# Moving scale and shift of the first norm behind the turn, for four of eight blocks

## The chip, the cores and the metric

The kernel runs on one core of a Trainium2 chip. The metric is the device time of one execution in microseconds (us). An execution under the profiler leaves a trace: every instruction of the engines TensorE (PE, its weight loads PEld), VectorE (DVE), ScalarE (ACT), GpSimd (POOL) and of SyncE's (SP) queue, which issues most transfers, with its start and end.

## The reference, cut to what matters

One layer of a decoder trunk on x of 1024 tokens by 1024 channels, in float32:

```python
x = _layer_norm(ALPHA * x + mixed, ln1_g, ln1_b)      # first norm
hid = silu(x @ w_ffn_gate) * (x @ w_ffn_up)           # 2816 hidden channels
x = _layer_norm(ALPHA * x + hid @ w_ffn_down, ln2_g, ln2_b)
```

`mixed` is the output of three branches (a state-space model, a gated recurrence, an attention), gated, summed and multiplied by `w_out`. A norm takes mean and variance over the 1024 channels of a token, divides, and then multiplies by a scale and adds a shift for each channel. The first norm's output is used twice: as the input of the two gate matrices, and as the residual of the second norm.

## The kernel before, in words

Every float32 operand of a product is split into a high and a low part, and a product is three matmuls (`mm3`, line 117 through `mm`). ScalarE casts the high part, VectorE subtracts to get the low part (`split`, lines 143 and 129). The three stages that matter here:

**Mix stage** (`mix_out`, from line 944). Tokens lie in eight blocks of 128, on the partitions; channels lie along a row. For each block `tb` and each half `dh` of the channels, 24 matmuls fill a PSUM bank, VectorE adds `ALPHA * x` and measures mean and variance (`measure`). After the second half `norm` (line 927) runs on VectorE: two passes subtract the mean and multiply by the scale row `g1`, a reciprocal, two passes multiply by 1/sigma and add the shift row `b1`. The scale and shift rows are broadcast to all partitions, since here a channel is a column. The result goes to DRAM (`x1_d`, through ScalarE's queue).

**Turn** (`turn`, from line 978). The gate stage needs channels on the partitions. TensorE transposes a normalised block in eight 128x128 pieces into two banks, `pa[0]` (channels 0 to 511) and `pa[1]` (512 to 1023). Blocks 0 to 3 are kept. Blocks 4 to 7 are combined with them into the operands `x22`, `s1` to `s4` of a seven-product scheme (Strassen's): ScalarE copies `pa[1]` to `x22`, VectorE subtracts and adds with `pa[0]` read straight from PSUM, VectorE or GpSimd does the other sums, and each operand is split (`operand`, line 970). Program order is: the second halves of blocks 4 to 7, each from block 5 on followed by the turn of the block before it; block 7 is turned inside the gate stage (line 1141), after three rounds of two products. The first product that needs an operand made from all of blocks 4 to 7 comes with `middle(0)`, line 1148.

**Down stage** (from line 1178). It multiplies the hidden values by `w_ffn_down`, in 7 products of 11 steps each, 12 matmuls a step. For each step SyncE loads two halves, ScalarE casts them and VectorE subtracts (`factors`); four such pairs of buffers exist, and three steps are prepared ahead. `residual(tb)` loads a block of the first norm's output back from `x1_d`; `scaled` multiplies it by ALPHA and adds a product; `finish` does the second norm, where ScalarE already subtracts the mean and divides in one pass (`Identity` with a scale and a bias for each partition).

What sets the order: a planner simulates the program and orders each engine's instructions by readiness and program order. From the gate stage on, compute instructions are pinned (`pin`): they keep their program order on their engine. Transfers are not pinned and are issued as early as their buffers and their queue allow. The down stage's buffers (`row`, `r`, `p3`) lie where those of the gate stage were, and wait for them.

Of the kernel before, what the change touches and what calls it, by code (L numbers as in the profile page):

```python
# [16 lines left out]
AF = mybir.ActivationFunctionType  # L17
ALU = mybir.AluOpType
# [3 lines left out]
P = 128  # L22
# [35 lines left out]
def trunk(ctx: ExitStack, tc: tile.TileContext, A: dict, out: bass.AP):  # L58
# [20 lines left out]

    LATE = {  # L80
        "ws": ("keep", 4), "w": ("keep", 8), "x": ("keep", 9), "m8": ("mid", 4), "ln": ("mid", 2),
        "mx": ("right", 8), "wo": ("right", 4), "r": ("down", 8), "row": ("down", 2), "p3": ("down", 22),
    }
    pinned = [False]
    count = [0]
# [12 lines left out]
    def small(shape, dt=F32, name_="c"):  # L98
        return const.tile(list(shape), dt, name=name(name_))
# [363 lines left out]
    PE.transpose(pr[:, 0:124], rows, ident[0:124, 0:124])  # L463
    cols = small([P, 124], name_="cols")
    DVE.tensor_copy(cols, pr[:, 0:124])
    half = small([P, 60], name_="half")
    ts(DVE, half, cols[:, 0:60], 0.5, ALU.mult)

# [458 lines left out]
    def norm(r, tb, g, b, ready=lambda dh: None):  # L927

        mv, rs = few("mv", [P, 4], 2, "const"), few("rs", [P, 1], 2, "const")
        pin(DVE.bn_aggr(mv[:, 0:2], stats.pop(tb)[:, :, 0:6]))  # L930
        pin(ACT.activation(rs, mv[:, 1:2], AF.Sqrt, bias=eps_t))
        for dh in range(2):
            pin(stt(r[dh], r[dh], mv[:, 0:1], g[dh], ALU.subtract, ALU.mult))
        pin(DVE.reciprocal(rs, rs))
        for dh in range(2):
            pin(stt(r[dh], r[dh], rs, b[dh], ALU.mult, ALU.add))
            ready(dh)

    def halves_of(t):
        return [t[:, 512 * dh : 512 * dh + 512] for dh in range(2)]  # L940

# [2 lines left out]
    def mix_out(tb, dh):  # L944
        h, c = tb // 4, slice((tb % 4) * P, (tb % 4 + 1) * P)
        if dh == 0:
            acc[tb] = new("x")
            SP.dma_start(acc[tb], x_in[tb * P : (tb + 1) * P, :])
        r = halves_of(acc[tb])
        ps = bank(tag="ba"[tb % 2])  # L950
        for k in range(NK):
            q, kk = k // 4, k % 4
            mm3(ps, MH[h][q][:, kk, c], ML[h][q][:, kk, c], WO[dh][q][0][:, kk, :], WO[dh][q][1][:, kk, :], k == 0, k == NK - 1)
        stt(r[dh], r[dh], ALPHA, ps, ALU.mult, ALU.add)
        measure(r[dh], tb, dh)
        if dh == 1:
            norm(r, tb, g1, b1)
            ACT.dma_start(x1_d[tb], acc[tb])


# [17 lines left out]
    def turn(tb, place, e=POOL):  # L978
        j = tb % 4
        pa = []  # L980
        for q in range(2):
            pa.append(place(q))
            for k in range(4):
                PE.transpose(pa[q][:, k, :], acc[tb][:, (4 * q + k) * P : (4 * q + k + 1) * P], ident)
        if tb < 4:
            raw[j] = new("x", shape=(P, 8, P))
            ACT.copy(raw[j][:, 0:4], pa[0])
            DVE.tensor_copy(raw[j][:, 4:8], pa[1])
            operand("x11", j, raw[j][:, 0:4], DVE)
            operand("x12", j, raw[j][:, 4:8], POOL)  # L990
            return
        xs, s1 = new("x", shape=(P, 8, P)), new("x", shape=(P, 8, P))[:, 0:4]
        x22, s2, s3, s4 = xs[:, 0:4], xs[:, 4:8], raw[j][:, 0:4], raw[j][:, 4:8]
        ACT.copy(x22, pa[1])
        tt(DVE, s3, s3, pa[0], ALU.subtract)
        tt(DVE, s1, pa[0], x22, ALU.add)
        tt(e, s2, x22, s3, ALU.subtract)
        tt(e, s4, s4, s2, ALU.subtract)
        operand("x22", j, x22, DVE)
        operand("s3", j, s3, DVE)  # L1000
        operand("s2", j, s2, e)
        operand("s1", j, s1, DVE)
        operand("s4", j, s4, e)
# [209 lines left out]
    def residual(tb):  # L1213
        t = new("r", shape=(P, D))
        SP.dma_start(t, x1_d[tb])
        whole[tb], res[tb] = t, halves_of(t)

    def scaled(tb, dh, e):
        pin(stt(res[tb][dh], res[tb][dh], ALPHA, e, ALU.mult, ALU.add))
# [3 lines left out]
        pin(measure(res[tb][dh], tb, dh))  # L1223

    def finish(tb, last=False):
        g2, b2 = rows_
        if last:
            norm(res[tb], tb, halves_of(g2), halves_of(b2), lambda dh: SP.dma_start(out[tb * P : (tb + 1) * P, 512 * dh : 512 * dh + 512], res[tb][dh]))
            return
        r = whole[tb]  # L1230
        mv, rs = few("mv", [P, 4], 2, "const"), few("rs", [P, 1], 2, "const")
        nm = mv[:, 2:3]
        pin(DVE.bn_aggr(mv[:, 0:2], stats.pop(tb)[:, :, 0:6]))
        pin(ACT.activation(rs, mv[:, 1:2], AF.Sqrt, bias=eps_t))
        pin(DVE.reciprocal(rs, rs))
        pin(ts(DVE, nm, mv[:, 0:1], rs, ALU.mult, -1.0, ALU.mult))
        pin(ACT.activation(r, r, AF.Identity, bias=nm, scale=rs))  # L1237
        tt(DVE, r, r, g2, ALU.mult)
        tt(POOL, r, r, b2, ALU.add)
        SP.dma_start(out[tb * P : (tb + 1) * P, :], r)  # L1240
# [59 lines left out]
    def measured(tb, dh):  # L1300
        pin(measure(res[tb][dh], tb, dh))

    for n in ("ln2_g", "ln2_b"):
        t = new("row", shape=(P, D))
        SP.dma_start(t, A[n].rearrange("(a d) -> a d", a=1).broadcast_to([P, D]))
        rows_.append(t)
# [43 lines left out]
```

## Time and profile before

| | us |
|---|---|
| median of 3 runs | 1650.58 (1650.56 to 1651.05) |
| the profiled execution | 1650.19 |
| its span, first to last instruction | 1648.4 |
| PE busy | 1592.8 |
| DVE busy | 1011.6 |
| ACT busy | 634.5 |
| POOL busy | 599.5 |

The mean granted clock of TensorE is 0.989 of full speed. Times in the rows are counted from the start of the span. The mix stage ends at 991, the gate stage runs from there to about 1424, the down stage to the end. In a row, the names are tiles without their numbers: `x` is a work tile, `ln` a broadcast row of the first norm, `mx`, `wo`, `m` hold split operands, `w` a split weight or hidden factor, `r` a residual block, `row` a broadcast row in the down stage, `p`, `a`, `b` are PSUM banks. `x3` at the end means three instructions merged into a row, the first figure their start and the second their length together.

### The profile page before, as it was taken

The page shows a single profiled execution, that of the slowest core. Times are in us where ns is not written, and L with a number is a line of the kernel's source. Part 1 is how long each engine was busy: PE and PEld are TensorE (multiplying, and loading weights), DVE is VectorE, ACT ScalarE, POOL GpSimd, SP SyncE. Part 2 cuts the span into 40 slices and gives each one's busy share as a digit, 9 for nine tenths or more (in the row PEclk, how much of TensorE's full clock was granted, in tenths as well). Part 3 has the DMA queues.
Part 4 walks back from the last instruction along what each step waited for, and adds up shares of the span by engine and source line. Part 5 has one row for each costly group of instructions (what it writes and reads, how often), then busy time and mean ns, then how long its engine had stood idle before and what let it go on. Part 6 is the DMA issues. An engine that isn't in the chain of part 4 may idle for free.

```text
span 1648.4 us, 20516 instructions
## 1 busy us (share of the span) xinstructions
PE 1592.8 (97%) x7482; PEld 1321.1 (80%) x7482; DVE 1011.6 (61%) x1602; ACT 634.5 (38%) x960; POOL 599.5 (36%) x529
## 2 busy tenths in 40 slices
PE   8989999999899999999999998999999999999997
PEld 6877888877787888888888886788888888778886
DVE  4756575723643467887657769666555555547766
ACT  4425454524633445564213224223222222244442
POOL 0111316333143011112040028599987888400004
PEclk9999999999999999999999998999999999999999
DMA  5343324333332333344754712356544455597752
GB/s 169 76 102 80 80 78 105 77 79 100 88 83 67 116 116 113 114 144 169 246 185 162 244 49 77 126 193 200 171 166 166 154 177 170 202 331 233 245 174 102
DMA packets 219968, 236.09 MB, mean 143 GB/s; under 512 B 33376, under 2 KB 162524, under 8 KB 219868
## 3 DMA queue, kind: packets, MB, share of 16 engines
q1 hardware_dynamic: 192604, 202.83, 39.5%
q10 hardware_dynamic: 27264, 31.96, 5.9%
q8 instruction: 59, 0.97, 0.2%
q14 instruction: 41, 0.34, 0.1%
HBM read 163.96 MB, written 70.78 MB: 142 GB/s over the span
## 4 chain that ended last, share of the span: by engine, by line
PE 78%; DVE 9%; issue 4%; DMA 3%; ACT 3%; POOL 2%; SPq 1%; ACTq 0%; DVEq 0%; POOLq 0%
PE b L117 35%; PE p L117 32%; PE a L117 8%; PE s L117 2%; PE a L341 1%; DMA ws<-w_ffn_down 1%; POOL s L129 1%; DVE r L129 1%; DVE s L129 1%; DVE x L137 1%; DVE wo L129 1%; DMA nck<-ck_d 1%; DVE m L129 1%; DVE x L129 1%; ACT r L1237 1%
## 5 line engine op out<-in xcount | busy, mean ns | idle before, releaser
L117 PE MATMUL b<-x,wh 128*128 128x512 f32 x912 | 351.9, 397 | 2.3 <-ACT s L708 1.7
L117 PE MATMUL b<-x,wl 128*128 128x512 f32 x832 | 328.5, 395 | 0.0
L117 PE MATMUL b<-m,wh 128*128 128x512 f32 x784 | 309.1, 394 | 0.0
L117 PE MATMUL p<-mx,w 128*128 128x512 f32 x1056 | 250.0, 392 | 2.1 <-DVE mx L129 1.3
L117 PEld LDWEIGHTS p<-mx,w 128*128 128x128 f32 x1056 | 199.7, 189 | 44.4 <-issue 1.7
L117 PEld LDWEIGHTS b<-x,wh 128*128 128x128 f32 x912 | 172.9, 190 | 37.4 <-ACT s L708 2.0
L117 PEld LDWEIGHTS b<-x,wl 128*128 128x128 f32 x832 | 157.4, 189 | 31.7
L129 DVE TENSOR_TENSOR x<-x,p 128x512 f32<-128x512 f32 x163 | 108.4, 683 | 109.4 <-PE p L117 92.5
L117 PEld LDWEIGHTS b<-m,wh 128*128 128x128 f32 x784 | 148.8, 190 | 28.7 <-issue 0.2
L117 PE MATMUL p<-w,w 128*128 128x512 f32 x528 | 157.4, 390 | 1.1 <-DVE w L129 1.0
L129 POOL TENSOR_TENSOR s<-s,s 128x1024 f32<-128x1024 f32 (+9 forms) x76 | 77.2, 1015 | 207.4 <-ACT s L852 75.2
L129 DVE TENSOR_TENSOR w<-ws,w 128x1024 fp32r<-128x1024 f32 x88 | 116.0, 1324 | 51.8 <-ACT w L143 51.6
L143 ACT CAST w<-ws 128x1024 fp32r<-128x1024 f32 x88 | 92.1, 1050 | 103.4 <-PE p L117 64.0
L117 PE MATMUL p<-wo,w 128*128 128x512 f32 x528 | 127.3, 389 | 0.0
L129 DVE TENSOR_TENSOR wl<-ws,wh 128x1024 fp32r<-128x1024 f32 x62 | 85.8, 1383 | 65.5 <-ACT wh L143 62.2
L117 PEld LDWEIGHTS p<-w,w 128*128 128x128 f32 x528 | 98.8, 188 | 22.9 <-DVE w L129 2.6
L117 PEld LDWEIGHTS p<-wo,w 128*128 128x128 f32 x528 | 99.1, 188 | 20.5
L143 ACT CAST wh<-ws 128x1024 fp32r<-128x1024 f32 x62 | 65.1, 1050 | 125.0 <-PE b L117 99.2
L129 DVE TENSOR_TENSOR w<-m,w 128x1024 fp32r<-128x1024 f32 x44 | 69.0, 1567 | 63.2 <-ACT w L143 63.2
L129 POOL TENSOR_TENSOR ln<-x,x 128x512 f32<-128x512 f32 x44 | 75.7, 1727 | 63.6 <-ACT x L1172 52.2
L117 PE MATMUL p<-w 128*128 128x512 f32 x264 | 97.5, 390 | 1.1 <-ACT w L143 1.1
L129 POOL TENSOR_TENSOR r<-r,row 128x1024 f32<-128x1024 f32 x7 | 16.7, 2391 | 189.5 <-DVE r L129 184.3
(276 smaller groups left out, 2721.6 us busy)
## 6 DMA issues: line engine op xcount, KB each, us to landing
ws<-w_in SPq DMA_DIRECT2D x48, 512.0 KB, 4.1
ws<-w_ffn_gate SPq DMA_DIRECT2D x27, 512.0 KB, 4.2
gate_d<-zs ACTq DMA_DIRECT2D x48, 256.0 KB, 2.0
zs<-gate_d SPq DMA_DIRECT2D x48, 256.0 KB, 2.8
ws<-w_ffn_up SPq DMA_DIRECT2D x22, 512.0 KB, 4.6
x<-w_ffn_down SPq DMA_DIRECT2D x22, 512.0 KB, 5.6
hid_d<-ln SPq DMA_DIRECT2D x22, 512.0 KB, 3.9
wts_d<-x SPq DMA_DIRECT2D x22, 512.0 KB, 2.6
```

Of the source, the lines that this page charges most:

```text
L117: PE.matmul(o, a, b, start=first, stop=last)
L129: return pin(e.tensor_tensor(o, a, b, op))
L137: return DVE.scalar_tensor_tensor(out=o, in0=a, scalar=s, in1=b, op0=op0, op1=op1)
L143: pin(ACT.copy(hi, src))
L341: PE.transpose(ta[:, j, e, :], pts[e][:, (k0 + j) * P : (k0 + j + 1) * P], ident)
L1237: pin(ACT.activation(r, r, AF.Identity, bias=nm, scale=rs))
```

## The change

Blocks 4 to 7 are normalised without scale and shift: a new function `center`, cut out of `finish`, does mean and 1/sigma with one pass of ScalarE, and `mix_out` calls it for these blocks in place of `norm`. What is stored in `x1_d` for them has no scale and shift. They are applied in two places. In `turn`, a channel is a partition, so ScalarE applies them as it reads the eight transposed pieces from PSUM, one instruction of 128x128 each, with the scale and shift of that piece as one value for each partition (`gain1`, `bias1`, loaded at the start with channels on the partitions); the first half goes to a new tile `x21`. In `residual`, GpSimd multiplies and adds the broadcast rows, which the down stage now loads as well (four `row` tiles instead of two). Blocks 0 to 3 are as before.

```diff
--- before.py
+++ after.py
@@ -79,7 +79,7 @@
 
     LATE = {
         "ws": ("keep", 4), "w": ("keep", 8), "x": ("keep", 9), "m8": ("mid", 4), "ln": ("mid", 2),
-        "mx": ("right", 8), "wo": ("right", 4), "r": ("down", 8), "row": ("down", 2), "p3": ("down", 22),
+        "mx": ("right", 8), "wo": ("right", 4), "r": ("down", 8), "row": ("down", 4), "p3": ("down", 22),
     }
     pinned = [False]
     count = [0]
@@ -463,6 +463,9 @@
     PE.transpose(pr[:, 0:124], rows, ident[0:124, 0:124])
     cols = small([P, 124], name_="cols")
     DVE.tensor_copy(cols, pr[:, 0:124])
+    gain1, bias1 = [small([P, 32], name_="gain")[:, 0:NK] for _ in range(2)]
+    for t, n in ((gain1, "ln1_g"), (bias1, "ln1_b")):
+        SP.dma_start(t, A[n].rearrange("(k p) -> p k", p=P))
     half = small([P, 60], name_="half")
     ts(DVE, half, cols[:, 0:60], 0.5, ALU.mult)
 
@@ -936,6 +939,16 @@
             pin(stt(r[dh], r[dh], rs, b[dh], ALU.mult, ALU.add))
             ready(dh)
 
+    def center(r, tb):
+
+        mv, rs = few("mv", [P, 4], 2, "const"), few("rs", [P, 1], 2, "const")
+        nm = mv[:, 2:3]
+        pin(DVE.bn_aggr(mv[:, 0:2], stats.pop(tb)[:, :, 0:6]))
+        pin(ACT.activation(rs, mv[:, 1:2], AF.Sqrt, bias=eps_t))
+        pin(DVE.reciprocal(rs, rs))
+        pin(ts(DVE, nm, mv[:, 0:1], rs, ALU.mult, -1.0, ALU.mult))
+        pin(ACT.activation(r, r, AF.Identity, bias=nm, scale=rs))
+
     def halves_of(t):
         return [t[:, 512 * dh : 512 * dh + 512] for dh in range(2)]
 
@@ -954,7 +967,10 @@
         stt(r[dh], r[dh], ALPHA, ps, ALU.mult, ALU.add)
         measure(r[dh], tb, dh)
         if dh == 1:
-            norm(r, tb, g1, b1)
+            if tb < 4:
+                norm(r, tb, g1, b1)
+            else:
+                center(acc[tb], tb)
             ACT.dma_start(x1_d[tb], acc[tb])
 
 
@@ -989,11 +1005,15 @@
             operand("x11", j, raw[j][:, 0:4], DVE)
             operand("x12", j, raw[j][:, 4:8], POOL)
             return
-        xs, s1 = new("x", shape=(P, 8, P)), new("x", shape=(P, 8, P))[:, 0:4]
-        x22, s2, s3, s4 = xs[:, 0:4], xs[:, 4:8], raw[j][:, 0:4], raw[j][:, 4:8]
-        ACT.copy(x22, pa[1])
-        tt(DVE, s3, s3, pa[0], ALU.subtract)
-        tt(DVE, s1, pa[0], x22, ALU.add)
+        xs, xt = new("x", shape=(P, 8, P)), new("x", shape=(P, 8, P))
+        x22, s2, s1, x21, s3, s4 = xs[:, 0:4], xs[:, 4:8], xt[:, 0:4], xt[:, 4:8], raw[j][:, 0:4], raw[j][:, 4:8]
+
+        for q, o in ((1, x22), (0, x21)):
+            for k in range(4):
+                c = slice(4 * q + k, 4 * q + k + 1)
+                ACT.activation(o[:, k, :], pa[q][:, k, :], AF.Identity, bias=bias1[:, c], scale=gain1[:, c])
+        tt(DVE, s3, s3, x21, ALU.subtract)
+        tt(DVE, s1, x21, x22, ALU.add)
         tt(e, s2, x22, s3, ALU.subtract)
         tt(e, s4, s4, s2, ALU.subtract)
         operand("x22", j, x22, DVE)
@@ -1214,6 +1234,9 @@
         t = new("r", shape=(P, D))
         SP.dma_start(t, x1_d[tb])
         whole[tb], res[tb] = t, halves_of(t)
+        if tb >= 4:
+            tt(POOL, t, t, rows_[2], ALU.mult)
+            tt(POOL, t, t, rows_[3], ALU.add)
 
     def scaled(tb, dh, e):
         pin(stt(res[tb][dh], res[tb][dh], ALPHA, e, ALU.mult, ALU.add))
@@ -1223,18 +1246,12 @@
         pin(measure(res[tb][dh], tb, dh))
 
     def finish(tb, last=False):
-        g2, b2 = rows_
+        g2, b2 = rows_[0:2]
         if last:
             norm(res[tb], tb, halves_of(g2), halves_of(b2), lambda dh: SP.dma_start(out[tb * P : (tb + 1) * P, 512 * dh : 512 * dh + 512], res[tb][dh]))
             return
         r = whole[tb]
-        mv, rs = few("mv", [P, 4], 2, "const"), few("rs", [P, 1], 2, "const")
-        nm = mv[:, 2:3]
-        pin(DVE.bn_aggr(mv[:, 0:2], stats.pop(tb)[:, :, 0:6]))
-        pin(ACT.activation(rs, mv[:, 1:2], AF.Sqrt, bias=eps_t))
-        pin(DVE.reciprocal(rs, rs))
-        pin(ts(DVE, nm, mv[:, 0:1], rs, ALU.mult, -1.0, ALU.mult))
-        pin(ACT.activation(r, r, AF.Identity, bias=nm, scale=rs))
+        center(r, tb)
         tt(DVE, r, r, g2, ALU.mult)
         tt(POOL, r, r, b2, ALU.add)
         SP.dma_start(out[tb * P : (tb + 1) * P, :], r)
@@ -1300,7 +1317,7 @@
     def measured(tb, dh):
         pin(measure(res[tb][dh], tb, dh))
 
-    for n in ("ln2_g", "ln2_b"):
+    for n in ("ln2_g", "ln2_b", "ln1_g", "ln1_b"):
         t = new("row", shape=(P, D))
         SP.dma_start(t, A[n].rearrange("(a d) -> a d", a=1).broadcast_to([P, D]))
         rows_.append(t)
```

## Rows read from the trace of the kernel before

**Rows 1.** The page's part 1: busy us of each engine, share of span, instructions.

```profile
PE 1592.8 (97%) x7482; PEld 1321.1 (80%) x7482; DVE 1011.6 (61%) x1602; ACT 634.5 (38%) x960; POOL 599.5 (36%) x529
```

**Rows 2.** TensorE's timeline at the seam: start, us, what, [idle before <-releaser].

```profile
985.39 5.71 PE L117 MATMUL a<-m,mx 128*128 128x512 f32 x24
...
996.90 1.09 PE L984 MATMUL b<-ident,x 128*128 128x128 f32 x4 [5.79 <-issue]
998.62 1.09 PE L984 MATMUL a<-ident,x 128*128 128x128 f32 x4 [0.63 <-DVE x L137]
1000.43 18.91 PE L117 MATMUL p<-mx,w 128*128 128x512 f32 x72 [0.73 <-ACT x L994]
...
1032.69 5.46 PE L117 MATMUL p<-mx,w 128*128 128x512 f32 x23 [1.32 <-DVE mx L129]
```

**Rows 3.** Windows at the seam: busy us per engine, granted clock, DMA share, GB/s.

```profile
993.00:998.00 5.00, 1.09 (x4) 0.71 (x4) 4.96 (x5) 0.00 (x0) 5.00 (x4) 0.71 0.00 0
998.00:1003.00 5.00, 3.65 (x10) 2.80 (x11) 5.00 (x7) 2.24 (x4) 3.71 (x3) 0.50 0.26 105
```

**Rows 4.** Timeline of all engines at the seam: VectorE's rows around block 6.

```profile
988.99 2.80 DVE L137 SCALAR_TENSOR_TENSOR x<-x,mv,ln 128x512 f32<-128x512 f32 x2
...
991.71 3.42 DVE L129 TENSOR_TENSOR wo<-x,wo 128x512 fp32r<-128x512 f32 x2
...
995.24 3.23 DVE L137 SCALAR_TENSOR_TENSOR x<-x,rs,ln 128x512 f32<-128x512 f32 x2
```

**Rows 5.** VectorE's groups by shape, 972 to 1045: xcount | busy us, mean ns | idle.

```profile
L137 DVE SCALAR_TENSOR_TENSOR x<-x,mv,ln 128x512 f32<-128x512 f32 x8 | 9.1, 1178 | 0.1
...
L137 DVE SCALAR_TENSOR_TENSOR x<-x,rs,ln 128x512 f32<-128x512 f32 x8 | 7.5, 976 | 0.1
```

**Rows 6.** Down stage: a window, SyncE's issues, and the page of DMA issues.

```profile
1450.00:1460.00 10.00, 10.00 (x45) 8.18 (x45) 2.45 (x2) 2.10 (x2) 0.00 (x0) 1.00 1.03 404
...
1449.31 1.50 SPq L1215 DMA_DIRECT2D r<-x_d  x2
...
r<-x_d SPq DMA_DIRECT2D x8, 512.0 KB, 8.7
```

**Rows 7.** Timeline of the tail: first and last step of a norm on ScalarE.

```profile
1610.99 0.19 DVE L1233 BATCH_NORM_AGGREGATE mv<-bn 128x2 f32<-128x12 f32 x1
...
1612.00 1.25 ACT L1237 ACTIVATE r<-r,mv,rs 128x1024 f32<-128x1024 f32 x1 [0.48 <-DVE mv L134]
```

**Rows 8.** Timeline at the seam: ScalarE's copy of a turned half, block 7.

```profile
1023.16 0.57 ACT L994 COPY x<-p 128x512 f32<-128x512 f32 x1
```

**Rows 9.** ScalarE: line 324 (ns min/median/max, first and last start), and a group.

```profile
L324 ACT ACTIVATE pt<-pt,st x64: 401/778/1157, 118.1 to 692.8; 128x128 f32<-128x128 f32 x8, 128x256 f32<-128x256 f32 x8, 128x384 f32<-128x384 f32 x8, 128x512 f32<-128x512 f32 x8
...
L1237 ACT ACTIVATE r<-r,mv,rs 128x1024 f32<-128x1024 f32 x7 | 8.7, 1244 | 3.4 <-DVE mv L134 3.4
```

**Rows 10.** GpSimd's and VectorE's timelines in the recurrence, GpSimd's in the tail.

```profile
742.25 2.75 POOL L129 TENSOR_TENSOR s<-s,s 128x1024 f32<-128x1024 f32 x1 [3.03 <-DVE s L850]
...
742.78 3.31 DVE L137 SCALAR_TENSOR_TENSOR s<-s,cols,s 128x1021 f32<-128x1021 f32 x1
...
1614.58 2.40 POOL L129 TENSOR_TENSOR r<-r,row 128x1024 f32<-128x1024 f32 x1 [178.24 <-DVE r L129]
```

**Rows 11.** Down stage: VectorE's splits, TensorE, a cast of ScalarE.

```profile
1457.75 1.23 DVE L129 TENSOR_TENSOR w<-ws,w 128x1024 fp32r<-128x1024 f32 x1 [5.39 <-ACT w L143]
...
1470.81 1.22 DVE L129 TENSOR_TENSOR w<-ws,w 128x1024 fp32r<-128x1024 f32 x1
...
1475.17 1.07 PE L117 MATMUL p<-w,w 128*128 128x512 f32 x4
...
1490.79 1.06 ACT L143 CAST w<-ws 128x1024 fp32r<-128x1024 f32 x1 [0.72 <-PE p L117]
```

**Rows 12.** Windows at the start, columns as in rows 3.

```profile
24.00:25.00 1.00, 0.59 (x5) 0.59 (x6) 0.00 (x0) 0.36 (x1) 0.00 (x0) 1.00 0.56 27
...
28.00:29.00 1.00, 1.00 (x6) 0.82 (x5) 0.00 (x0) 0.00 (x0) 0.00 (x0) 1.00 0.03 8
```

## The prediction

> **What bounds the kernel now.** I read the part on busy time first. TensorE is busy 97% of the span, every other engine 61% or less [rows 1]. So a change of this kind is worth what it does to TensorE's few stalls, and I looked for stalls near the lines of the diff. The first place is the seam between the mix stage and the gate stage, read in TensorE's timeline: 24 matmuls take 5.71 us up to 991.1, then TensorE is idle 5.79 us until it can turn block 6, 0.63 us more between the two halves of that turn, and 0.73 us before the first product [rows 2]. In the windows the granted clock falls to 0.71 and then to 0.50 there, the lower of its two levels, 1.2 of 2.4 GHz [rows 3], and the 72 matmuls that follow take 18.91 us. A last stall of 1.32 us stands at 1032.69 [rows 2].
>
> Why it waits 5.79 us stands in the timeline of all engines: the first two normalising passes of block 6 on VectorE start at 988.99 and take 2.80 us, two splits of block 4's operands go in between (3.42 us), and the second two passes run from 995.24 for 3.23 us [rows 4]. GpSimd is busy 5.00 of 5.00 us meanwhile [rows 3]. Over the seam, where GpSimd is at work too, the means of these passes are 1.18 and 0.98 us, 16.6 us for 16 [rows 5].
>
> The second place is the start of the down stage. In its window the DMA engines are busy 1.03 at 404 GB/s [rows 6], because the residual blocks are fetched there as early as the queue allows (two of blocks 4 to 7 issued at 1449.31, median 8.7 us to landing). There VectorE's splits reach TensorE just in time.
>
> **The change at the seam.** It removes the four passes per block, 16.6 us of VectorE in all, and adds the chain that the second norm has already: from aggregation to the end of the scalar engine's pass is 1610.99 to 1613.25, 2.3 us [rows 7]. Block 6 would then be ready at about 991 instead of 998.5. TensorE wants it at 991.1. ScalarE has block 5's pieces ahead of it in the queue (below), so I leave 1.0 us of the 5.79: -4.8 us (ends: 0 and -5.8). The 0.63 us goes, since both halves become ready together: -0.6.
>
> ACT.copy of one half (0.57 us [rows 8]) becomes four pieces of 128x128 with two pointer operands, and the other half, which VectorE read straight from PSUM, becomes four more. No row has such a piece. The nearest: a 128x128 activation with one pointer 401 ns, and at 1024 wide 1157 ns with one pointer against 1244 with two [rows 9], so 87 ns for a pointer and some 490 ns for a piece; eight take 3.9 us end to end, which is the upper end, and the lower is the 0.57 us of the copy they replace. I take 3.2, near the upper row, with a little overlap of neighbours. The bank of the first product is released by four of them, not by one copy: the 0.73 us grows by 1.0 (0 to 1.4). Subtraction and addition behind them now have two SBUF operands, as the passes of [rows 5], and pay more when GpSimd works; I put that in the next figure. Block 7 is turned last, and the operand behind the 1.32 us stall is made from it; eight pieces in place of a copy lengthen its chain by 2.6 us, some of which the relieved VectorE gives back: +2.0 (0 to +4.2).
>
> If the idle stretch shrinks to about 2 us, the clock should stay up: behind the 1.32 us stall 23 matmuls take 5.46 us, full pace [rows 2]. Three runs of 24 at 5.71 us, less their overlaps, are 16.9 us against 18.91: -2.0. The two transposes of 1.09 us at a low clock halve: -1.1. Ends: 0 and -3.1.
>
> Seam: -4.8 - 0.6 + 1.0 + 2.0 - 2.0 - 1.1 = **-5.5 us** (ends: all gains and no new cost, -9.5; nothing gained and both costs, +5.6).
>
> No row shows the Identity function while Silu's table is loaded, which block 7 may meet. The Trainium skill, "ScalarE: Activation LUTs", section "Table sets: the hidden batching unit", says that cheap functions such as identity "appear in *every* set as filler"; by it no table load is added. No run here shows it yet.
>
> **The change in the down stage.** Blocks 4 to 7 come back without scale and shift, so GpSimd multiplies and adds them: 8 passes of 128x1024 by a broadcast row. The like in the tail takes 2.40 us [rows 10]. GpSimd has nothing else there until the tail, so nothing queues behind them; but they start when the blocks land, from about 1458 to 1459, and nothing holds them back. What they meet is VectorE. At 742.25 a GpSimd pass starts, at 742.78 a VectorE pass of the same width with two SBUF inputs, and it ends at 746.09, 1.09 us after GpSimd's: it waited 2 us for the other [rows 10]. The splits that TensorE waits for are such passes, 1.23 us alone [rows 11].
>
> In the trace of before a split starts at 1457.75, the fifth after it at 1470.81, and TensorE uses that one from 1475.17 [rows 11]. With GpSimd alternating, from 1459.0 on: 8 passes of 2.0 to 2.4 us, 5 splits of 1.1 us and the 3 scaled residual halves between them at 0.6: 23.3 to 26.5 us, so the fifth split is done at 1482.3 to 1485.5, and TensorE is 7.1 to 10.3 us late. I take **+8.5 us**. If the blocks land later, splits have a lead: at 1490.79 the cast itself waits for TensorE to free a buffer [rows 11], all four pairs of buffers being full: three steps of 12 matmuls, half of 5.71 us each, are some 8 us of lead, and the cost goes to 0. Ends: 0, and 13 with a lower clock in the new gaps (10.3, and about what the seam loses to it now, 3.1).
>
> By the Trainium skill, "SBUF — State Buffer", section "Who interferes with whom", whoever starts first keeps the shared port pair for its whole instruction and the other fully blocks. The pair of rows at 742 agrees (1.09 us left after GpSimd's end). By the rule taken at its full 2.40 us, this term would be 10.3 and the sum 1.8 higher.
>
> Two more broadcast rows, 1 MB, are 2.6 us of DMA at 404 GB/s, in or just ahead of the full stretch. While VectorE is late the DMA engines catch up, so most hides behind the term before: +1.0 (0 to 2.6); without that cover it is 2.6.
>
> **The rest.** The two loads at the start have 1024 elements of 4 bytes each. The nearest stretch, 24 to 25 us, moves small pieces at 27 GB/s with the engines 0.56 busy, and at 28 to 29 the engines rest at 0.03 [rows 12]. A few us of pieces fit in that rest: 0 (up to 2 if the weight load behind them is late). The planner draws up the order of all stages anew, and it can shift through these; no row prices that, and it stays in the range. The tail's code is the same.
>
> **Sum.** -5.5 + 8.5 + 1.0 = +4.0 us on the profiled execution's 1650.19 (span 1648.4 and 1.8 around it): 1654.2. The median of the runs is 0.4 above that execution, so I predict 1654.6. About 0.2%, 3.3 us, is what a measurement of this kernel tells from no change.
>
> **Rivals.**
> - *GpSimd's passes meet full buffers* (faster). If the blocks of 4 to 7 land after about 1485, or the passes are issued later, splits have 8 us of lead and the down stage costs 0 to 1.5 us. Then -5.5 + 1.5 = -4.0, some 1646.6 (1641 to 1649.5). It decides at the landing of block 4: before 1475 it costs, after 1485 not. Against it: the first two are issued at 1449.31 already [rows 6], though the code asks for them much later. For it: two more loads and new places in memory. Chance 0.28.
> - *The stall at the seam stays.* ScalarE gets 3.2 us of pieces and 1.25 us of norm [rows 7] per block, besides its casts, in some 6 us of TensorE work. If block 6's norm waits behind them, the 5.79 us stays in other words and the clock falls as before; then +1.0 + 2.0 at the seam and 9.5 down: 1661 to 1663. For it: the order of ScalarE's queue is the planner's. Against: the norm stands earlier in the code. Chance 0.12.
> - *Both partly.* The passes cost 4 to 7 us and the seam gives back as much: 1648 to 1653.8, no difference to be seen. Chance 0.15.
> - Forecast: chance 0.45, own range 1651 to 1661; a tenth of it lies within 0.2%.
>
> Faster 0.28; same 0.15 + 0.05 = 0.20; slower 0.40 + 0.12 = 0.52. Range 1643 to 1662: it takes in most of the faster rival and leaves out about 2 in 10.
>
> **What would show it.** At the seam: block 6's turn starts within 2 us of the matmuls' end, and the clock stays at 1.00 in the windows (right), or the gap stays above 4 us (wrong). Pieces of 0.45 to 0.5 us. In the down stage: eight GpSimd passes of 2.4 us or more in one run soon after 1455, splits of 3 us among them, and TensorE waiting for VectorE's `w`; if the splits stay at 1.23 us or TensorE runs through, that step is wrong. A total below 1650 would make the prediction wrong in sign.

## The result and the profile after

The changed kernel takes 1665.37 us (median of 6 runs, 1662.61 to 1666.37) against 1650.82 us for the kernel before on the same chip: ratio 1.0085, 95% interval 1.0072 to 1.0097. So it is slower, as forecast, by some 14 us instead of 4. The profiled execution took 1664.37 us with a span of 1662.5.

The page's first part for the changed kernel answers to [rows 1]: TensorE is still nearly the whole span, VectorE is busy 4 us less, ScalarE 13 and GpSimd 26 us more.

```profile
PE 1599.6 (96%) x7482; PEld 1326.3 (80%) x7482; DVE 1007.8 (61%) x1590; ACT 647.8 (39%) x992; POOL 625.6 (38%) x537
```

To place the 14.1 us of span I cut the trace at two TensorE rows that every kernel here has: the start of the 24 matmuls that precede turn 4, and a wait of about 1 us for VectorE's `w` late in the gate stage. First TensorE's timeline of the kernel before at these two, then that of the changed kernel.

```profile
972.75 5.61 PE L117 MATMUL a<-m,mx 128*128 128x512 f32 x24
...
1426.32 2.13 PE L117 MATMUL p<-w,w 128*128 128x512 f32 x8 [0.98 <-DVE w L129]
```

```profile
972.74 5.61 PE L117 MATMUL a<-m,mx 128*128 128x512 f32 x24
...
988.31 0.66 PE L1000 MATMUL b<-ident,x 128*128 128x128 f32 x4 [3.60 <-ACT x L950]
...
989.19 7.28 PE L117 MATMUL a<-m,mx 128*128 128x512 f32 x24
996.30 0.60 PE L1000 MATMUL b<-ident,x 128*128 128x128 f32 x4
...
999.74 18.05 PE L117 MATMUL p<-mx,w 128*128 128x512 f32 x72 [2.40 <-ACT x L1014]
...
1032.45 0.73 PE L117 MATMUL p<-mx,w 128*128 128x512 f32 x2 [2.90 <-ACT mx L991]
...
1428.40 1.88 PE L117 MATMUL p<-w,w 128*128 128x512 f32 x7 [0.99 <-DVE w L129]
```

From the first row to the last is 453.57 us before and 455.66 after: the seam, forecast at -5.5, costs **+2.1**. From there to the end of the span is 222.08 before (1648.4 - 1426.32) and 234.10 after: the down stage, forecast at +9.5, costs **+12.0**.

The seam first. Against [rows 2], block 6's wait of 5.79 and 0.63 us is gone: its transposes at 996.30 follow the matmuls at once. But a new wait of 3.60 us stands one block earlier, in front of block 5's transposes, and block 7's 24 matmuls behind it take 7.28 us instead of 5.71. VectorE's rows there, and then ScalarE's, show what block 5's norm waited for.

```profile
979.84 0.21 DVE L946 BATCH_NORM_AGGREGATE mv<-bn 128x2 f32<-128x12 f32 x1
982.19 1.29 DVE L129 TENSOR_TENSOR x<-x,x 128x512 f32<-128x512 f32 x2 [2.15 <-ACT x L1014]
983.40 0.16 DVE L948 RECIPROCAL rs<-rs 128x1 f32<-128x1 f32 x1
983.48 3.38 DVE L129 TENSOR_TENSOR wo<-x,wo 128x512 fp32r<-128x512 f32 x2
986.78 0.20 DVE L134 TENSOR_SCALAR mv<-mv,rs 128x1 f32<-128x1 f32 x1
...
1009.61 0.15 DVE L948 RECIPROCAL rs<-rs 128x1 f32<-128x1 f32 x1
...
1013.00 0.20 DVE L134 TENSOR_SCALAR mv<-mv,rs 128x1 f32<-128x1 f32 x1
```

```profile
979.26 1.50 ACT L1014 ACTIVATE x<-a,gain,gain 128x128 f32<-128x128 f32 x4 [2.61 <-DMA x_d<-x]
980.64 1.52 ACT L1014 ACTIVATE x<-b,gain,gain 128x128 f32<-128x128 f32 x4
982.01 0.33 ACT L947 ACTIVATE rs<-mv,eps 128x1 f32<-128x1 f32 x1
...
987.01 1.24 ACT L950 ACTIVATE x<-x,mv,rs 128x1024 f32<-128x1024 f32 x1 [3.48 <-DVE mv L134]
...
1023.64 0.64 ACT L1092 ACTIVATE x<-x 128x512 f32<-128x512 f32 x1 [1.33 <-DVE x L129]
1024.17 2.88 ACT L1014 ACTIVATE x<-p,gain,gain 128x128 f32<-128x128 f32 x8
```

The norm is now a relay between the two engines, of steps under 0.35 us and a last pass of 1.24 us, and turn 4's longer instructions stand between the steps. The aggregate is ready at 980.05. The square root starts at 982.01, behind the eight pieces. The reciprocal follows two sums at 983.40, the scaling two splits of 3.38 us together at 986.78. The normalising pass ends at 988.25, when block 6's matmuls have been done since 984.7. Block 7 meets the same on VectorE: a reciprocal at 1009.61, two splits, and its scaling only at 1013.00.

Now the down stage: GpSimd's, VectorE's and TensorE's rows of the changed kernel.

```profile
1464.00 23.52 POOL L129 TENSOR_TENSOR r<-r,row 128x1024 f32<-128x1024 f32 x8 [25.57 <-DMA r<-x_d]
```

```profile
1473.00 2.86 DVE L137 SCALAR_TENSOR_TENSOR r<-r,x 128x512 f32<-128x512 f32 x1
1475.78 3.40 DVE L129 TENSOR_TENSOR w<-ws,w 128x1024 fp32r<-128x1024 f32 x1
...
1487.99 1.21 DVE L129 TENSOR_TENSOR w<-ws,w 128x1024 fp32r<-128x1024 f32 x1
1489.13 0.68 DVE L137 SCALAR_TENSOR_TENSOR r<-r,x 128x512 f32<-128x512 f32 x1
```

```profile
1470.25 1.96 PE L117 MATMUL p<-w 128*128 128x512 f32 x4 [3.10 <-ACT w L143]
1473.13 3.78 PE L117 MATMUL p<-w,w 128*128 128x512 f32 x8 [0.92 <-DVE w L129]
1479.24 2.11 PE L117 MATMUL p<-w,w 128*128 128x512 f32 x8 [1.20 <-DVE w L129]
1485.33 2.11 PE L117 MATMUL p<-w,w 128*128 128x512 f32 x8 [3.07 <-DVE w L129]
1489.26 2.12 PE L117 MATMUL p<-w,w 128*128 128x512 f32 x8 [0.92 <-DVE w L129]
```

The eight passes run in one go, and while they do a split takes 3.40 us instead of 1.21 and a scaled half 2.86 instead of 0.68. TensorE's five waits add up to 9.21 us, and its matmuls at the lower clock to 2.4 more (eight in 3.78 us against 2.11 further down, four in 1.96 against 1.20 for the like at 1463.80). Four of the waits are for VectorE's `w`. The first, 3.10 us, is for ScalarE's cast, and that is a late load, as ScalarE's row shows, and the windows behind it (columns as in [rows 3]): the DMA engines are full up to 1470. The clock of 0.66 stands behind both the seam's wait and this one.

```profile
1469.15 1.04 ACT L143 CAST w<-ws 128x1024 fp32r<-128x1024 f32 x1 [3.46 <-DMA ws<-w_ffn_down]
```

```profile
988.00:993.00 5.00, 4.69 (x18) 3.95 (x19) 0.89 (x4) 3.29 (x7) 0.00 (x0) 0.66 0.52 210
...
1460.00:1470.00 10.00, 6.53 (x26) 4.30 (x25) 2.32 (x2) 3.84 (x6) 5.92 (x3) 1.00 1.04 399
1470.00:1480.00 10.00, 7.63 (x19) 5.30 (x20) 9.77 (x4) 4.38 (x5) 9.84 (x4) 0.66 0.30 104
```

### The profile page after: what moved, and what is told of

Read it like the earlier page. It is cut to its first block, busy times and chain, and to the rows that moved or that the text cites. A ratio compares the mean times of both kernels' runs of the same rounds, so it can differ in the third digit from the quotient of the medians.

```text
span 1662.5 us, 20547 instructions
## 1 busy us (share of the span) xinstructions
PE 1599.6 (96%) x7482; PEld 1326.3 (80%) x7482; DVE 1007.8 (61%) x1590; ACT 647.8 (39%) x992; POOL 625.6 (38%) x537
## 5 line engine op out<-in xcount | busy, mean ns | idle before, releaser
L129 DVE TENSOR_TENSOR w<-ws,w 128x1024 fp32r<-128x1024 f32 x88 | 120.3, 1373 | 54.7 <-ACT w L143 54.6
L117 PEld LDWEIGHTS p<-w,w 128*128 128x128 f32 x528 | 99.7, 190 | 30.6 <-DVE w L129 10.3
L129 POOL TENSOR_TENSOR r<-r,row 128x1024 f32<-128x1024 f32 x15 | 39.9, 2672 | 178.3 <-DVE r L129 152.5
```

The source lines that it names most:

```text
L117: PE.matmul(o, a, b, start=first, stop=last)
L129: return pin(e.tensor_tensor(o, a, b, op))
```

## The experiments

The theories at the start. **A**: in the down stage GpSimd's passes alternate with VectorE's splits while TensorE has no lead. **B**: the transfers are what costs there, the two rows and the early residual blocks. For the seam: **S1**, block 5's small steps queue behind turn 4's work; **S2**, it is the length of the pieces, or the whole work of the two engines, in whatever order.

The table has each kernel's median, its ratio to the kernel before as measured beside it, and the two stretches of its profiled span, cut as above.

| kernel | us | ratio (95%) | seam | rest |
|---|---|---|---|---|
| before | 1650.8 to 1652.2 | 1 | 453.57 | 222.08 |
| changed | 1665.37 | 1.0085 (1.0072 to 1.0097) | 455.66 | 234.10 |
| e1_no_pass | 1655.99 | 1.0024 (1.0010 to 1.0037) | 454.55 | 225.50 |
| e2_seam_only | 1653.69 | 1.0002 (0.9992 to 1.0013) | 455.44 | 222.15 |
| e3_before_passes | 1662.32 | 1.0053 (1.0037 to 1.0070) | 456.30 | 232.54 |
| e4_late_load | 1654.52 | 1.0013 (1.0002 to 1.0023) | 456.19 | 224.16 |
| e7_copies | 1651.29 | 1.0000 (0.9990 to 1.0010) | 454.63 | 222.49 |
| e6_order_late | 1658.58 | 1.0040 (1.0025 to 1.0055) | 458.81 | 224.10 |
| e9_spread | 1659.67 | 1.0044 (1.0025 to 1.0064) | 458.81 | 225.42 |
| e10_order5 | 1648.84 | 0.9985 (0.9975 to 0.9994) | 448.97 | 224.34 |
| e11_turn_late | 1652.11 | 1.0002 (0.9990 to 1.0014) | 453.20 | 223.56 |
| e13_order5_dve | 1646.05 | 0.9966 (0.9953 to 0.9980) | 446.83 | 224.17 |
| e14_order5_early | 1656.93 | 1.0024 (1.0014 to 1.0034) | 448.24 | 233.72 |

The same code at the seam came out within some 2.7 us: 453.57 and 456.30 (e3_before_passes) as before, 454.55 to 456.19 as changed. Up to the down stage the engines run the same instructions in the same order in both traces with the seam of before, so this is not the planner's doing. The scatter lies behind the start of the gate stage: from the first cut to there it is 27.68 us in both of them, and 26.83 to 27.02 in the four as changed. So 0.7 us is gained up to the gate stage, and the seam's +2.1 as a whole is no larger than the scatter: no gain shows there, and the time of e2_seam_only (ratio 1.0002) says the same. Only differences well above it are read below. The rest repeats within 0.8 us where its code is the same (222.08 to 222.49; 223.56 to 224.34; 233.72 and 234.10).

### The down stage

**e1_no_pass**: the change without GpSimd's passes (the residual of blocks 4 to 7 goes without scale and shift); the rows are still loaded.

```diff
-        if tb >= 4:
-            tt(POOL, t, t, rows_[2], ALU.mult)
-            tt(POOL, t, t, rows_[3], ALU.add)
```

> The changed kernel without GpSimd's eight passes in the down stage; the two extra broadcast rows are still loaded. It leaves out scale and shift of the residual of blocks 4 to 7. Theory A (the passes take turns with VectorE's splits while TensorE has no lead): of the 12 us that the down stage lost, some 9 go and the 3.1 us wait for a late load at 1470 stays: 1655 to 1657. Rival B (the two extra rows and the later residual loads make the weight loads late, and the passes only fill the gaps): 1663 or more. Splits of 1.2 us in both.

**e2_seam_only**: the two extra rows are gone as well, and there are two `row` tiles again.

```diff
-    for n in ("ln2_g", "ln2_b", "ln1_g", "ln1_b"):
+    for n in ("ln2_g", "ln2_b"):
```

> The changed kernel without the passes and without the two extra rows: the down stage of before, the seam of after. It leaves out scale and shift of the residual of blocks 4 to 7. Theory A: before plus the 2.1 us by which the gate stage ends later: 1652 to 1654. Against e1 it tells the price of the two rows: 3 us if the late load at 1470 comes from them. Rival C (the seam did gain, and the planner lost it elsewhere): below 1648. A fault of the early loads would show as a time above 1656.

Without the passes the rest falls from 234.10 to 225.50 us, so the passes cost **8.6**; without the rows it falls to 222.15, so the rows cost **3.4** and nothing is left to explain (before: 222.08). Whole runs put the two at 9.4 and 2.3 us by the medians, 10.1 and 3.6 by the ratios. The times of e1_no_pass and e2_seam_only lie in the ranges of theory A. TensorE's timeline without passes keeps the wait for the cast and loses all four for VectorE:

```profile
1470.57 1.84 PE L117 MATMUL p<-w 128*128 128x512 f32 x4 [3.08 <-ACT w L143]
```

**e3_before_passes**: the kernel before with eight such passes on its residual blocks 4 to 7 (by the second norm's rows, which are loaded anyway; so its residual is another one), and nothing else.

```diff
         whole[tb], res[tb] = t, halves_of(t)
+        if tb >= 4:
+            tt(POOL, t, t, rows_[0], ALU.mult)
+            tt(POOL, t, t, rows_[1], ALU.add)
```

> The kernel before plus eight GpSimd passes of 128x1024 on the residual blocks 4 to 7 in the down stage, with the two rows that are there already (it scales and shifts these residuals by the second norm's rows, which the reference doesn't). No extra load, no change at the seam. Theory A: splits of 3.4 us while the passes last, and 8 to 11 us more than before: 1659 to 1662. Rival B: GpSimd's passes cost nothing by themselves: 1650 to 1652.

The rest grows by 10.46 us, and TensorE's new waits are all for VectorE. One of the four is shown. The time, 1662.32, is 0.3 us above the range of theory A.

```profile
1470.04 3.58 PE L117 MATMUL p<-w,w 128*128 128x512 f32 x8 [1.87 <-DVE w L129]
```

**e4_late_load**: the whole change, with the residual loads of blocks 4 to 7 held behind the weight loads.

```diff
-            SP.dma_start(t[:, e], src[2 * j + b][:, c])
+            done["f"] = SP.dma_start(t[:, e], src[2 * j + b][:, c])
...
-        SP.dma_start(t, x1_d[tb])
+        with after(done["f"] if tb >= 4 else None):
+            SP.dma_start(t, x1_d[tb])
```

> The whole computation as changed, but the residual loads of blocks 4 to 7 keep their place in SyncE's queue behind the weight loads, so they land near 1495 and later, one block every few steps, and the passes follow them there. Theory A with lead: the splits are three steps ahead by then, the passes cost 0 to 2 us and the 2 MB leave the full DMA stretch: 1650 to 1654. Theory A without the lead mattering (each pass costs its share wherever it falls): 1659 or more.

The same eight passes, 28 us later, and the same two rows now cost 2.1 us together (224.16 against 222.08); the time, 1654.52, is 0.5 us above the range forecast for a lead. GpSimd's row, one of VectorE's, and the longest of TensorE's three waits, 2.25 us in all:

```profile
1491.73 26.27 POOL L129 TENSOR_TENSOR r<-r,row 128x1024 f32<-128x1024 f32 x8 [53.68 <-DMA ws<-hids_d]
```

```profile
1496.23 2.83 DVE L129 TENSOR_TENSOR w<-ws,w 128x1024 fp32r<-128x1024 f32 x1
```

```profile
1512.47 0.73 PE L117 MATMUL p<-w,w 128*128 128x512 f32 x2 [1.61 <-DVE w L129]
```

VectorE is slowed here too (2.83 us for this split), but for 20 us TensorE lives on splits made ahead. The wait for the late cast is gone too. So theory A holds for 8.6 to 10.5 of the 12 us, and B for the 3.4 that the rows cost: they are issued ahead of the residual blocks, into DMA engines that are already full. It takes both to make the load late: without the rows (e2_seam_only) and without the early residual blocks (e4_late_load) that wait is gone.

### The seam

**e7_copies**: e2_seam_only with two copies in place of the eight pieces, so without scale and shift in the turned blocks.

```diff
-            for k in range(4):
-                c = slice(4 * q + k, 4 * q + k + 1)
-                ACT.activation(o[:, k, :], pa[q][:, k, :], AF.Identity, bias=bias1[:, c], scale=gain1[:, c])
+            ACT.copy(o, pa[q])
```

> The seam kernel (no row passes, no extra rows in the down stage: 1653.69 us, TensorE stalls of 3.60, 2.40 and 4.32 us around the last blocks of the mix stage) with the eight pieces of ScalarE of each turned block replaced by two plain copies of 512 columns, as before the change; the scale and shift of the first norm are left out for blocks 4 to 7, in the turned blocks and in the residual. Theory S1 (block 5's norm is late because its small instructions queue behind whatever of turn 4 stands ahead of them, on ScalarE and on VectorE, and because VectorE's splits beside GpSimd take 3.4 us): the copies are some 0.8 to 1.2 us shorter in all than the pieces, the 3.60 us stall stays within 2.4 to 3.6 us, and the time within 1651.5 to 1654. Theory S2 (the length of the pieces on ScalarE is the stall): the stall falls below 1.5 us, TensorE keeps its clock in the next blocks, and the time is 1648 to 1650.

TensorE's wait for block 5 is 1.81 us, between the two theories, and the time, 1651.29, just below S1's range: it told nothing apart. The row:

```profile
986.05 0.66 PE L1000 MATMUL b<-ident,x 128*128 128x128 f32 x4 [1.81 <-ACT x L950]
```

ScalarE is done with the two copies 1.8 us sooner than with the pieces, and the wait is 1.8 us shorter: the pieces are a link of the chain too, ahead of the square root and of the sums. The first product's bank then waits 0.68 us instead of 2.40. The gate stage starts 5.1 us sooner behind the first cut than in e2_seam_only (21.90 us against 27.02), but two waits at block 7's operand, 3.56 and 3.48 us, take most of it back.

**e6_order_late**: e4_late_load with each of turns 4, 5 and 6 ordered behind the norm of the block after it.

```diff
+            with after(done["dve", 4 + j]), after(done["act", 4 + j]):
                 turn(3 + j, old)
```

(`done` holds the scaling on VectorE and the normalising pass of each block.)

> The whole computation, with the residual loads of blocks 4 to 7 kept behind the weight loads (as in the run of 1654.52 us) and, new, the eight pieces, the sums and the splits of turned blocks 4 to 6 ordered behind the norm of the block after on ScalarE and VectorE. Theory S1 (queue order): the 3.60 us stall in front of block 5's transposes falls to below 1 us and the 24 transposes and matmuls behind it take 5.7 us again instead of 7.3; the operands of the turned blocks come about 1.5 us later, and the 2.40 us stall behind them may stay; the time is 4 to 5 us below the late-load kernel's, 1649 to 1651. Theory S2 (ScalarE's and VectorE's total work between the blocks is the bound, whatever its order): the stall moves on to blocks 6, 7 or to the first matmuls of the gate stage, and the time stays within 1653 to 1656.

Both theories missed the time, 1658.58 us. Block 5's wait is gone, as S1 has it, but a stall has moved on to the first matmuls of the gate stage, as S2 has it, and it is far longer than the one that went. TensorE's row, and VectorE's rows that explain it:

```profile
1005.52 19.30 PE L117 MATMUL p<-mx,w 128*128 128x512 f32 x72 [13.42 <-ACT x L1014]
```

```profile
999.27 0.15 DVE L948 RECIPROCAL rs<-rs 128x1 f32<-128x1 f32 x1
999.34 1.67 DVE L129 TENSOR_TENSOR wo<-x,wo 128x512 fp32r<-128x512 f32 x1
1000.93 1.74 DVE L129 TENSOR_TENSOR mx<-x,mx 128x512 fp32r<-128x512 f32 x1
1002.60 0.20 DVE L134 TENSOR_SCALAR mv<-mv,rs 128x1 f32<-128x1 f32 x1
```

Block 7's reciprocal, which stands behind two splits already, is followed by two more before the scaling, and turn 6, which empties the last bank, had been told to wait for them. It is the same queue two blocks on, and my order made TensorE wait for it.

**e10_order5**: only turn 4 is ordered behind block 5's norm (`if j == 1`).

```diff
+            with after(done["dve", 5] if j == 1 else None), after(done["act", 5] if j == 1 else None):
                 turn(3 + j, old)
```

> The whole computation with the residual loads of blocks 4 to 7 late (1654.52 us without an order) and only turn 4 ordered behind the norm of block 5, on ScalarE and VectorE; turns 5 and 6 are free again. With all three turns ordered (1658.58 us) the 3.60 us stall was gone, but a stall of 13.42 us stood in front of the gate stage, since block 7's reciprocal and scaling queued behind the four splits of turns 4 and 5 on VectorE (999.27 and 1002.60 us) and turn 6 had to wait for it. Theory S1' (a turn may only be held behind a norm whose small instructions are themselves ahead of the splits): the 3.60 us stall goes, the next eight blocks of matmuls run in 5.7 us, the 13.42 us is about 2.4 us again; the time is 4 to 5 us below the late-load kernel's, 1649 to 1651. Rival S2' (splits and pieces that were put off come back as a stall of the same size at the gate stage): 1653 to 1656.

**e11_turn_late**: turn 5 stands behind block 7's matmuls as well, and turns 5 and 6 behind block 7's norm.

```diff
-        if j:
-            turn(3 + j, old)
+        if j % 2:
+            with after(done["dve", 4 + j]), after(done["act", 4 + j]):
+                turn(3 + j if j == 1 else 5, old)
+                if j == 3:
+                    turn(6, old)
```

> As the kernel before it, and the transposes of turn 5 moved behind block 7's matmuls, with turns 5 and 6 ordered behind the norm of block 7 on ScalarE and VectorE, so that block 6's norm is hidden behind block 7's matmuls and block 7's small instructions stand ahead of every split of turns 5 and 6. Theory S1': no stall before block 7's matmuls end; then one of about 2.5 to 4 us while block 7's norm (aggregate, square root, reciprocal, scaling, 1.25 us normalisation) runs and turns 5 and 6 are turned and emptied (16 pieces, 6 us in two halves); the gate stage starts at 997 to 999.5 us against 998.86, and the time is 1651 to 1654. Rival S2': the 16 pieces in one go empty the banks later than 1001 us, and the time is above 1655.

The order of turn 4 alone takes 7.2 us from the seam (456.19 to 448.97; whole runs put it at 4.6 by the ratios): 1648.84 us, below the kernel before. Some 3 of the 7.2 us stand ahead of the gate stage. The wait of 2.9 us behind block 7 is gone, and a new one of 2.35 us stands in front of block 6's transposes. TensorE's rows, and VectorE's that explains the new one: with turn 4 held back on both engines, two of its splits now stand ahead of block 6's reciprocal, which follows only at 992.82.

```profile
994.55 0.65 PE L1000 MATMUL b<-ident,x 128*128 128x128 f32 x4 [2.35 <-ACT x L950]
...
997.85 19.35 PE L117 MATMUL p<-mx,w 128*128 128x512 f32 x72 [2.21 <-ACT x L1014]
```

```profile
989.55 3.35 DVE L129 TENSOR_TENSOR wo<-x,wo 128x512 fp32r<-128x512 f32 x2
```

e11_turn_late comes in its range, 1652.11, and shows the price of emptying both turns at the end: a wait of 7.23 us in front of the gate stage, which starts at 999.58.

**e13_order5_dve**: as e10_order5, ordered on VectorE alone; on ScalarE the pieces stand ahead of the square root again.

```diff
-            with after(done["dve", 5] if j == 1 else None), after(done["act", 5] if j == 1 else None):
+            with after(done["dve", 5] if j == 1 else None):
```

> The whole computation with late residual loads, and turn 4 ordered behind the norm of block 5 on VectorE alone; on ScalarE the eight pieces of turn 4 stand ahead of block 5's square root again. In the changed kernel block 5's norm was aggregated at 979.84 and scaled at 986.78: 2.2 us of that until ScalarE had done the pieces, 1.4 us behind the two sums, 3.4 us behind the two splits on VectorE. Theory V (VectorE's queue, 4.3 us of the delay, is what makes the 3.60 us stall; the pieces' 1.7 us fit into the 5.7 us of matmuls of block 6): the stall is 0 to 0.5 us and the time 1648 to 1650.5, that of the kernel ordered on both engines (1648.84). Rival P (the pieces on ScalarE are the delay that counts): the stall stays above 2 us and the time is 1652 to 1655.

The rival falls, and the time is better than my theory asked: 1646.05 us, 0.34% below the kernel before (interval 0.20 to 0.47%). VectorE's rows of block 5's norm, then TensorE's seam:

```profile
978.40 0.21 DVE L946 BATCH_NORM_AGGREGATE mv<-bn 128x2 f32<-128x12 f32 x1
980.95 0.16 DVE L948 RECIPROCAL rs<-rs 128x1 f32<-128x1 f32 x1 [2.34 <-ACT rs L947]
981.14 0.21 DVE L134 TENSOR_SCALAR mv<-mv,rs 128x1 f32<-128x1 f32 x1
```

```profile
983.91 5.70 PE L117 MATMUL a<-m,mx 128*128 128x512 f32 x24
989.70 0.66 PE L1000 MATMUL b<-ident,x 128*128 128x128 f32 x4
...
994.57 18.17 PE L117 MATMUL p<-mx,w 128*128 128x512 f32 x72 [3.78 <-ACT x L1014]
```

The 2.34 us that VectorE waits for the square root, behind the pieces, are hidden behind block 6's matmuls; aggregate to scaling is 2.7 us instead of 6.9, and TensorE goes from 977.5 to 990.8 with hardly a gap. The splits of turn 4 also come before block 6's norm again, and block 6's wait is gone too. So for block 5's wait it is enough to take the sums and splits (4.7 us) out of the chain; the pieces may stay ahead of the square root. They are not free: the first product's bank waits 3.78 us for them here.

**e14_order5_early**: e10_order5 with the residual loads where the change has them (`SP.dma_start(t, x1_d[tb])` without the order).

> The changed kernel with turn 4 ordered behind the norm of block 5 on both engines and the residual loads where the change left them (early). The order of the seam's instructions is the one of the kernel of 1648.84 us, that of the down stage the one of the changed kernel. If the two corrections are independent, the seam keeps its 4 to 5 us gain over the kernel before, the down stage its 12 us loss: the stretch from block 5's matmuls to the wait of about 1 us near the end of the gate stage takes 448 to 450 us (455.66 changed, 453.57 before), the rest 233 to 235 us, the time is 1657 to 1660. If the down stage's loss came from the seam (another phase of the queues, a clock that stays low), it falls below 8 us and the time below 1655.

The seam keeps its gain (448.24), the down stage its loss (233.72); the time, 1656.93, is just below the range. The two corrections are independent, as far as one trace of each shows.

**e9_spread**: e6_order_late with residual blocks 4 and 5 asked for behind product 2, 6 and 7 behind product 6.

```diff
-            todo.append(partial(residual, 4 + tb))
+            if tb < 2:
+                todo.append(partial(residual, 4 + tb))
     def after_6(Q):
+        for tb in (6, 7):
+            todo.append(partial(residual, tb))
```

> The kernel with the norm's order and the late loads, with the residual passes spread: blocks 4 and 5 are loaded behind product 2, blocks 6 and 7 behind product 6, instead of all four behind product 2. Where the two-way alternation of GpSimd's passes with VectorE's splits eats a lead of TensorE that lasts about two splits, half as many passes in a row leave the lead standing: the waits of 2.25 us in all at 1512 to 1519 us go, and the time is 1 to 3 us below the kernel with the order alone. Where each pass costs what it takes from VectorE, whenever it runs (about 2.0 us a pass over the splits beside it, all through), the total is unchanged to 0.5 us.

No gain: the rest is 225.42 us against 224.10. The three small waits became one, of 2.68 us at 1539.53, behind the second group of passes. Spreading did not help, but the rest, 1.3 us longer, did not stay within 0.5 us either, so neither expectation is met.

## Why the prediction was wrong

**Seam, the wait of block 6: the step that failed.** "I leave 1.0 us of the 5.79: -4.8 us" is right for block 6, where nothing is left, but no step asked whether the new chain, ScalarE and VectorE in turn, would hold up another block. Before, block 5's norm did not stop TensorE; now it waits 3.60 us, and the clock that falls there makes block 7's matmuls 1.6 us longer. Both stood at nothing in my sum. I looked for a queue ahead of block 6 on ScalarE ("block 5's pieces ahead of it in the queue"), and it was block 5's reciprocal and scaling behind two sums and two splits on VectorE. Up to the start of the gate stage I had -5.5 (-4.8, -0.6, +1.0 and -1.1); the trace has -0.7 (27.00 us from the first cut against 27.68). With that queue put right, e13_order5_dve has a seam of -6.7 us, 4.4 of them ahead of the gate stage (23.27 us against 27.68): the gain was there, and the order of one engine's queue took it away. The rival "the stall at the seam stays" (0.12, 1661 to 1663) came nearest, for another block and on another engine than it named.

**The bank of the first product** waits 2.40 us instead of 0.73: +1.7 against +1.0. Eight pieces take 2.88 us (3.2 forecast): one is 0.46 us long, as forecast, but neighbours overlap to 0.36 each. So the pieces were well bounded.

**Block 7's chain**: +2.0 forecast. From the end of its transposes the next 84 matmuls take 24.29 us with their wait (1018.41 to 1042.70) instead of 20.74 (1019.97 to 1040.71): +3.55, of which the longer wait (2.90 against 1.32) is 1.6 and the clock behind it most of the rest. How much of this is the change's own stays open: e3_before_passes has the seam's code of before, with the engines' instructions in the same order, and its wait there is 2.94 us and its seam 2.7 us longer. VectorE's last two splits ahead of that wait, before and in e3_before_passes, and TensorE's row in the latter:

```profile
1031.26 1.28 DVE L129 TENSOR_TENSOR mx<-x,mx 128x512 fp32r<-128x512 f32 x2
```

```profile
1031.53 3.43 DVE L129 TENSOR_TENSOR mx<-x,mx 128x512 fp32r<-128x512 f32 x2
1035.10 7.10 PE L117 MATMUL p<-mx,w 128*128 128x512 f32 x23 [2.94 <-DVE mx L129]
```

In e3_before_passes GpSimd's sums beside them start 1.0 us later behind the first cut, at 1016.49, for a weight load that landed late, and the splits meet GpSimd's passes that they missed in the trace of before. Why the load was late stays open.

**The clock**: -2.0 forecast for the 72 matmuls; they take 18.05 us instead of 18.91, so -0.9, and block 7's 24 give 1.6 back. The clock did not stay at 1.00, as the forecast asked: it is 0.66 from 988 to 993.

**Table load**: the pieces at 1024.17 run straight behind Silu, with no load between them. That agrees with the Trainium skill, "ScalarE: Activation LUTs", section "Table sets: the hidden batching unit".

**Down stage, the passes**: +8.5 forecast, 8.6 measured as the difference of e1_no_pass, 10.5 alone in e3_before_passes, against ends of 7.1 and 10.3 for the alternation. The mechanism was right and its size about right, and so was the remark that with some 8 us of lead the cost goes towards 0: it is 2.1 in e4_late_load, rows included. That 8.6 meets 8.5 so closely is luck: in the changed kernel the passes start at 1464.00 instead of 1459, and VectorE, idle until 1470.23 for the late cast, is not delayed by the first two. Alone, without the late cast, the passes cost what the upper end says.

**Down stage, the two rows**: "+1.0 (0 to 2.6)" was mis-sized; they cost 3.4. I let the rows hide behind VectorE's lateness. They delay a weight block that TensorE needs *before* the passes begin to matter, so the two costs mostly follow each other: alone they are 10.5 and 3.4, together 12.0, so only some 1.8 us hid. The window of 1460 to 1470 with DMA engines busy 1.04 shows that nothing could be caught up there.

**Sum.** Seam 7.6 us worse than forecast and down stage 2.5 make the 10 us. The two errors have one sign, and the range's upper end came from a single rival, not from both stages going wrong together.

## What to carry to other kernels

Moving a norm from four long passes on one engine to a relay of small steps on two shortens the work, but each step now waits in a queue of its own: count, for every block and not for the one that waits today, what stands in each engine's queue between two steps. Holding one turn's work back on one engine and loading later turned +14 us into -6 here (1646.05 against 1652.19). A slow pass on GpSimd beside VectorE is to be placed where the consumer has work in store: 28 us later the same eight passes cost 2 us with the two rows, instead of 12.

## What the runs showed of the hardware

While GpSimd's eight passes run (2.92 us each on average there), a VectorE instruction with two SBUF inputs was longer by the same 2.2 us at both lengths: 3.40 for 1.21 at 1475.78, 2.86 for 0.68 at 1473.00. So the shorter one suffers more in proportion, and the cost there goes with the number of such instructions rather than with their length. This agrees with the Trainium skill, "SBUF — State Buffer", section "Who interferes with whom", by which a VectorE instruction with two SBUF inputs contends with a GpSimd instruction that reads SBUF, and the lock on the ports that they share is exclusive.

The wait in front of the 72 matmuls does not tell by its length what the clock does behind it. Behind 2.40 us the granted clock (a window's mean of the two levels, 0.50 and 1.00) is 1.00 from 998 to 1003 in e1_no_pass and e2_seam_only, and the matmuls took 16.62 us; behind the same 2.40 us it is 0.66 in that window in the changed kernel, and they took 18.05. Behind 2.21 us in e10_order5 it is 0.50 there and they took 19.35, behind 13.42 us in e6_order_late they took 19.30. In the first two, as in the changed kernel, the clock had been low before, behind block 5's wait (0.66 to 0.71 from 988 to 993). What decides was not tried.
